# SSD stage of a hybrid SSD and chunk-MLP mixer: products from states in float32r parts, row tiles loaded by direction

## The chip, the cores and the metric

The kernel runs on one core of one Trainium2 chip. The metric is the device time in microseconds of one execution. The engines are named as in the profile: PE is TensorE (matmuls), PEld its weight loads, DVE VectorE, ACT ScalarE, POOL GpSimd, SP SyncE. L12 is line 12 of the kernel.

## The reference, cut to what matters

One layer of a mixer: a joint input projection of 256 latent and 256 context tokens (2,048 wide), a bidirectional SSD (32 heads of 64, in 8 groups of 4 heads, state 128, chunks of 128 tokens) beside a chunked gating MLP, and an output projection. Context tokens only provide the states from which the latent scans start. The part that the change touches, for one direction:

```
a = dtc * A;  acs = jnp.cumsum(a, axis=2);  a_tot = acs[:, :, -1]
decay_to_end = jnp.exp(a_tot[:, :, None] - acs)
states = einsum('bckgn,bckgr,bckgrp->bcgrpn', Bc, decay_to_end, xdt)
hT, h_starts = lax.scan(step, h0, (states, a_tot))     # h * exp(at) + s
CB = einsum('bcqgn,bckgn->bcgqk', Cc, Bc)
Lmat = exp(where(mask, acs_q - acs_k, -inf))
y_diag = einsum('bcgqk,bcgrqk,bckgrp->bcqgrp', CB, Lmat, xdt)
y_off = einsum('bcqgn,bcgrpn,bcqgr->bcqgrp', Cc, h_starts, exp(acs))
```

x, B and C come out of the projection through a depthwise convolution of 5 taps and silu. All is float32.

## The kernel before

The kernel has four stages one after another: adaLN and the first tiles of the projection (to about 126 us), the **SSD stage** (to about 440 us), the latent blocks, and the output projection. The change touches the SSD stage alone.

**Weight tiles.** The stage walks over 25 tiles of the projection (`REST`, i = 4 to 11, 14, 16 to 27, 30, 28, 29, 31), each of 128 output channels. Tile i belongs to group i // 4; i % 4 says what it holds: 0 and 1 are the two x tiles of the group, 2 is B, 3 is C (latent tokens only: 256 columns, the others 512). Tiles 12, 13 and 15 were computed earlier. One tile is 48 matmuls into a bank `psx` (two banks, used in turn): for each of 16 k steps three products in float32r parts, hi·hi (L140), hi·lo (L141) and lo·hi (L142). A weight tile is split in halves of 8 k steps, the hi part by ACT (`split_hi`, L542), the lo part by DVE (`split_lo`, L548, raw minus hi), three halves ahead of use. Halves are numbered through: tile 10 uses `w12` and `w13`.

**What sets the order.** Nothing is scheduled by the machine: each engine runs its instructions in the order in which the program issues them. Small jobs are put in a queue with a due time in units (`later`), and `pump` issues those that are due after each pair of k steps: 1.3 units for six matmuls of 512 columns, 0.65 for six of 256. So a due time fixes beside which matmuls of the projection a job stands, and on every engine the job waits behind what was issued before it. `plan_tile` (L975) gives the due times of a tile: tap 0 on ACT (L607), the other taps on DVE (L623), silu on ACT (L626), and what belongs to the group.

**A group's work**, in the order of due times after its C tile:

- `ssd_cb`: C by B for the latent chunks, PE into `pcb` (L851); `ssd_cbm`: its two masked copies `cbb` and `cbf` by DVE (L859, L860).
- `ssd_states`: context states, PE into `psc` (L868, B by the weighted x `xw`, two fp32 products of 512 columns), and states of the latent chunks into `psl` (L871).
- `ssd_hc` (ACT, L878, `hs` from `psc`), `ssd_hd` (POOL, L884), `ssd_hl` (DVE, L890): the start states `hs`.
- `ssd_mb` (POOL, L896) and `ssd_m` (DVE, L904 and L906), once per chunk: M, and E times M in place. M of the second chunk takes the buffer of the first, and yc that one again.
- `ssd_o`: C by `hs`, PE into `pso` (L920, two fp32 products of 512 columns); `ssd_yo` (DVE, L926) and `ssd_ya` (POOL, L934) take them out.
- `ssd_yd`: x by E, PE into `psy` (L946); `ssd_yc`, `ssd_yt`, `ssd_yf` turn it and add it to y.

**E.** `row_load` (POOL's DMA, L724) brings the running sums of a group, broadcast over 128 partitions, from DRAM (`acs`) into a tile `R` of 1 MB, both directions in one. ACT adds the negative column sums (`ssd_d`, L820), DVE takes the minimum of the two directions into a tile `E` (`ssd_min`, L827), ACT takes Exp (`ssd_e`, L833). This runs a group ahead: `plan_d` and `plan_e` are due 11 and 17 units after the C tile of the group before. Exp and silu lie in different tables of ACT, so each change costs an ACT_TABLE_LOAD.

`xw` and `xl` (x weighted for the states) are made by POOL (`ssd_w`, L785; `ssd_wl`, L792).

Of the kernel before, what the change touches and what calls it, by code (L numbers as in the profile page):

```python
# [47 lines left out]
def tile_hybrid_ssd_mlp(  # L48
# [688 lines left out]
    def turn(T, src, nm):
        nc.vector.transpose(T.rearrange("p (b g c) -> p g b c", b=4, g=4), src.rearrange("p (g b c) -> p g b c", g=4, b=4))
# [40 lines left out]
    def ssd_w(g):  # L779
        S = gs_[g]  # L780
        h4 = slice(4 * g, 4 * g + 4)
        xw = cv1.tile([P, 2, 2, 256], F32, tag="xw", name=f"xw{g}")
        for t in range(2):
            for d in range(2):
                nc.gpsimd.tensor_tensor(hx(xw[:, t, d, :]), xtok_(g, t), hb(wctx(t, d)[:, h4]), op=ALU.mult)  # L785
        S["xw"] = xw

    def ssd_wl(g):
        h4 = slice(4 * g, 4 * g + 4)
# [32 lines left out]

    def ssd_min(g, c):
        R = rows_[g]
        if c == 0:
            gs_.setdefault(g, {})["E"] = cv1.tile([P, 2, 4, P], F32, tag="E", name=f"E{g}")
        nc.vector.tensor_tensor(gs_[g]["E"][:, c], R[:, :, 0, c, :], R[:, :, 1, c, :], op=ALU.min)  # L827
        if c == 1:
            later(12 if g == 4 else 0, lambda: row_load(g + 1))

    def ssd_e(g):
# [1 line left out]
        nc.scalar.activation(E, E, AF.Exp)  # L833
# [28 lines left out]

    def ssd_states(g):
        S = gs_[g]
        bk, xw, xl = S["bk"], S["xw"], S["xl"]
        psc = spt([P, 2, 256], f"psc{g}")
        for t in range(2):
            nc.tensor.matmul(psc, lhsT=bk[:, t, :], rhs=xw[:, t], start=t == 0, stop=t == 1)  # L868
# [31 lines left out]
    def ssd_m(g, c):  # L900
        S = gs_[g]
        E, M = S["E"], S["M"]
        for h in range(4):
            nc.vector.scalar_tensor_tensor(M[:, h, :], S["cbf"][:, c, :], dtt[:, 3 * c, 4 * g + h : 4 * g + h + 1],  # L904
                                           M[:, h, :], op0=ALU.mult, op1=ALU.add)
        nc.vector.tensor_tensor(E[:, c], M, E[:, c], op=ALU.mult)  # L906
# [8 lines left out]
    def ssd_o(g):  # L915
        S = gs_[g]
        ct, hs = done[4 * g + 3], S["hs"]
        S["pso"] = [spt([P, 2, 256], f"pso{g}{c}") for c in range(2)]
        for c in range(2):
            nc.tensor.matmul(S["pso"][c], lhsT=ct[:, c * P : (c + 1) * P], rhs=hs[:, c], start=True, stop=True)  # L920
# [17 lines left out]
    def ssd_yd(g):  # L938
        S = gs_[g]
        E, xk = S["E"], S["xk"]  # L940
        ps = spt([P, 2, 2, P], f"psy{g}")
        for c in range(2):
            for q in range(2):
                for hh in range(2):
                    h = 2 * q + hh
                    nc.tensor.matmul(ps[64 * hh : 64 * hh + 64, c, q, :], lhsT=xk[:, q, 2 + c, hh * 64 : (hh + 1) * 64],  # L946
                                     rhs=E[:, c, h, :], start=True, stop=True)
# [467 lines left out]
```

## Time and profile before

| | |
|---|---|
| median of 3 runs | 962.25 us (961.64 to 963.29) |
| profiled execution, its own time | 962.39 us |
| its span | 960.6 us |
| granted clock | 0.998 |
| matmul records | 5,128 |

The page gives busy time of each engine over the span; the rows of the timeline give the start in us from the span's start, the duration, the engine with its line, the operation, output and inputs by name, the tile, and in brackets how long the engine had stood idle and what ended that. A row with x4 stands for four records run together. For the eight groups the timeline gives these starts of the products (us), and the end of the second E:

| group | pcb | psc | pso | second E done | psy |
|---|---|---|---|---|---|
| 0 | 169.1 | 169.5 | 178.9 | 184.5 | 184.9 |
| 1 | 196.0 | 196.5 | 205.9 | 207.8 | 211.8 |
| 2 | 241.7 | 242.2 | 251.6 | 253.0 | 258.9 |
| 3 | 269.6 | 270.0 | 279.7 | 281.6 | 285.7 |
| 4 | 303.1 | 303.6 | 311.6 | 314.9 | 318.9 |
| 5 | 347.6 | 348.0 | 356.1 | 358.7 | 363.3 |
| 6 | 392.0 | 392.5 | 400.5 | 403.8 | 407.8 |
| 7 | 422.0 | 422.4 | 432.7 | 437.3 | 438.6 |

### The profile page before, as it was taken

The page shows a single profiled execution, that of the slowest core. Times are in us where ns is not written, and L with a number is a line of the kernel's source. Part 1 is how long each engine was busy: PE and PEld are TensorE (multiplying, and loading weights), DVE is VectorE, ACT ScalarE, POOL GpSimd, SP SyncE. Part 2 cuts the span into 40 slices and gives each one's busy share as a digit, 9 for nine tenths or more (in the row PEclk, how much of TensorE's full clock was granted, in tenths as well). Part 3 has the DMA queues.
Part 4 walks back from the last instruction along what each step waited for, and adds up shares of the span by engine and source line. Part 5 has one row for each costly group of instructions (what it writes and reads, how often), then busy time and mean ns, then how long its engine had stood idle before and what let it go on. Part 6 is the DMA issues. An engine that isn't in the chain of part 4 may idle for free.

```text
span 960.6 us, 13754 instructions
## 1 busy us (share of the span) xinstructions
PE 950.8 (99%) x5128; PEld 769.6 (80%) x5128; DVE 675.0 (70%) x1108; ACT 481.8 (50%) x728; POOL 192.1 (20%) x294
## 2 busy tenths in 40 slices
PE   9999999999999999999999999999999999999997
PEld 4688888778787878787888888888888888888885
DVE  6888899889787776676766776766666665445636
ACT  4344358565564544455445443455665554355522
POOL 0000002423424324243000000043445440000000
PEclk9999999999999999999999999999999999999999
DMA  9999967468668667467787777786666666556722
GB/s 366 418 415 416 365 232 203 124 167 190 168 148 224 146 205 160 143 180 258 296 304 283 261 275 294 269 304 215 220 219 211 228 211 215 186 190 243 267 88 87
DMA packets 149970, 225.63 MB, mean 235 GB/s; under 512 B 119296, under 2 KB 119552, under 8 KB 127248
## 3 DMA queue, kind: packets, MB, share of 16 engines
q1 hardware_dynamic: 142992, 207.08, 64.0%
q0 software_dynamic: 6336, 16.86, 5.3%
q8 instruction: 40, 0.66, 0.3%
q10 hardware_dynamic: 576, 0.82, 0.2%
q14 instruction: 26, 0.21, 0.1%
HBM read 211.29 MB, written 9.25 MB: 230 GB/s over the span
## 4 chain that ended last, share of the span: by engine, by line
PE 93%; DVE 3%; DMA 2%; issue 1%; POOL 1%; ACT 0%; SPq 0%; POOLq 0%; ACTq 0%
PE pa L1192 12%; PE pa L1191 12%; PE pa L1193 12%; PE psx L140 9%; PE psx L142 9%; PE psx L141 9%; PE pm L1232 3%; PE pm L1233 3%; PE pm L1234 3%; PE pq L1234 2%; PE pq L1232 2%; PE pq L1233 2%; PE psada L253 2%; DMA ada<-in_wada_dram 1%; PE pso L920 1%; PE psc L868 1%
## 5 line engine op out<-in xcount | busy, mean ns | idle before, releaser
L87 DVE TENSOR_TENSOR lo_w<-w,hi_w 128x1024 fp32r<-128x1024 f32 x173 | 209.8, 1221 | 133.8 <-ACT hi_w L86 133.7
L86 ACT CAST hi_w<-w 128x1024 fp32r<-128x1024 f32 x173 | 181.9, 1053 | 206.4 <-PE pa L1193 138.1
L1191 PE MATMUL pa<-hi_w,hhi 128*128 128x512 f32 x512 | 200.5, 392 | 0.0
L1193 PE MATMUL pa<-hi_w,hlo 128*128 128x512 f32 x512 | 199.3, 389 | 0.0
L1192 PE MATMUL pa<-lo_w,hhi 128*128 128x512 f32 x512 | 199.2, 389 | 0.0
L140 PE MATMUL psx<-hhi,hi_w 128*128 128x512 f32 (+1 forms) x400 | 151.3, 378 | 1.0 <-DVE xbc L623 1.0
L142 PE MATMUL psx<-hhi,lo_w 128*128 128x512 f32 (+1 forms) x400 | 145.6, 364 | 0.0
L141 PE MATMUL psx<-hlo,hi_w 128*128 128x512 f32 (+1 forms) x400 | 145.6, 364 | 0.0
L1191 PEld LDWEIGHTS pa<-hi_w,hhi 128*128 128x128 f32 x512 | 96.1, 188 | 20.2 <-issue 0.4
L1193 PEld LDWEIGHTS pa<-hi_w,hlo 128*128 128x128 f32 x512 | 96.1, 188 | 20.0
L1192 PEld LDWEIGHTS pa<-lo_w,hhi 128*128 128x128 f32 x512 | 96.1, 188 | 19.9 <-issue 0.2
L548 DVE TENSOR_TENSOR lo_w<-w,hi_w 128x1024 fp32r<-128x1024 f32 x61 | 76.9, 1268 | 17.1 <-ACT hi_w L542 17.0
L623 DVE SCALAR_TENSOR_TENSOR xbc<-psx,pc,xbc 128x248 f32<-128x248 f32 (+1 forms) x204 | 83.3, 471 | 7.7 <-ACT xbc L607 6.9
L140 PEld LDWEIGHTS psx<-hhi,hi_w 128*128 128x128 f32 x400 | 75.4, 189 | 15.5 <-issue 3.1
L141 PEld LDWEIGHTS psx<-hlo,hi_w 128*128 128x128 f32 x400 | 75.5, 189 | 13.0 <-issue 1.7
L542 ACT CAST hi_w<-w 128x1024 fp32r<-128x1024 f32 x61 | 63.4, 1043 | 44.6 <-PE psx L141 30.8
L142 PEld LDWEIGHTS psx<-hhi,lo_w 128*128 128x128 f32 x400 | 75.4, 189 | 12.2
L1232 PE MATMUL pm<-hi_w,hhi 128*128 128x512 f32 x128 | 49.8, 389 | 0.0
L1233 PE MATMUL pm<-lo_w,hhi 128*128 128x512 f32 x128 | 49.8, 389 | 0.0
L1234 PE MATMUL pm<-hi_w,hlo 128*128 128x512 f32 x128 | 49.8, 389 | 0.0
L1071 DVE SCALAR_TENSOR_TENSOR junk<-gate,cb 128x2048 bf16<-128x2048 f32 x16 | 36.6, 2291 | 18.4 <-DMA gate<-in_wada_dram 18.4
L1096 POOL DMA_DIRECT2D y<-T x64 | 36.9, 584 | 47.6 <-ACT sq L1167 32.6
(268 smaller groups left out, 1405.7 us busy)
## 6 DMA issues: line engine op xcount, KB each, us to landing
w<-in_wlat_dram SPq DMA_DIRECT2D x64, 1024.0 KB, 4.9
w<-in_wout_dram SPq DMA_DIRECT2D x32, 1024.0 KB, 4.8
w<-in_wxbc_dram SPq DMA_DIRECT2D x25, 1024.0 KB, 6.6
ada<-in_wada_dram SPq DMA_DIRECT2D x24, 1024.0 KB, 13.7
gate<-in_wada_dram SPq DMA_DIRECT2D x16, 1024.0 KB, 5.4
ada<-in_wada_dram SPq DMA_DIRECT2D x16, 512.0 KB, 12.4
R<-acs POOLq DMA_DIRECT2D x8, 1024.0 KB, 7.2
wst<-in_wst_dram SPq DMA_DIRECT2D x15, 480.0 KB, 12.9
```

The source lines that it names most:

```text
L86: nc.scalar.copy(hi, raw)
L87: nc.vector.tensor_tensor(lo, raw, hi.bitcast(F32), op=ALU.subtract)
L140: nc.tensor.matmul(ps, lhsT=whi, rhs=hhi[k][:, s], start=start, stop=False)
L141: nc.tensor.matmul(ps, lhsT=whi, rhs=hlo[k][:, s], start=False, stop=False)
L142: nc.tensor.matmul(ps, lhsT=wlo, rhs=hhi[k][:, s], start=False, stop=stop)
L623: nc.vector.scalar_tensor_tensor(ao, zi, cw[:, k : k + 1], ao, op0=ALU.mult, op1=ALU.add)
L1191: nc.tensor.matmul(pa[tk], lhsT=hhi[k][:, t], rhs=whi[:, w], start=k == 0, stop=False)
L1192: nc.tensor.matmul(pa[tk], lhsT=hhi[k][:, t], rhs=wlo[:, w], start=False, stop=False)
L1193: nc.tensor.matmul(pa[tk], lhsT=hlo[k][:, t], rhs=whi[:, w], start=False, stop=k == KT - 1)
L1232: nc.tensor.matmul(p, lhsT=yh[:, t], rhs=whi[:, w], start=j == 0, stop=False)
L1233: nc.tensor.matmul(p, lhsT=yh[:, t], rhs=wlo[:, w], start=False, stop=False)
L1234: nc.tensor.matmul(p, lhsT=yl[:, t], rhs=whi[:, w], start=False, stop=hf == 0 and j == 15)
```

## The change

1. **Rows by direction.** `acs` holds the two directions apart, and `row_load(g, d)` fills one of two tiles R0, R1 of 512 KB. There is no tile E: the minimum and Exp are written in place in R0. R1 of the next group is loaded after the minima, R0 only after psy of this group. The biases of R1 are due at 11 units as before, those of R0 at 24, the minima and Exp at 28.5 (before 17).
2. **States** of groups 1 to 6 as three float32r products: `xw` and B are split by a new `hi_lo` (ACT copy to the hi part, L800 of the new file; DVE subtracts it for the lo part, L801).
3. **Outputs from states** of groups 1, 2, 4, 5, 6 as three float32r products: C and `hs` are split in the same way. Their pso, yo and ya are due 8 units later, behind psy.
4. **Due times**: `late` of tile 7 is 18 (14), of tile 15 it is 20 (17); in group 1 `xl` and the skip term come 3 later, in group 3 `xw` 1.5 later.

The diff, cut to its core:

```diff
-        R = cv1.tile([P, 4, 2, 2, P], F32, tag="R", name=f"R{g}")
...
+        R = cv1.tile([P, 4, 2, P], F32, tag=f"R{d}", name=f"R{d}_{g}")
+        nc.gpsimd.dma_start(R.rearrange("p h c q -> p (h c q)"),
+                            acs[d, 4 * g : 4 * g + 4, :].rearrange("h x -> (h x)").unsqueeze(0).partition_broadcast(P))
+        rows_[g, d] = R
...
+    def out_parts(g):
+        return g in (1, 2, 4, 5, 6)
+
+    def state_parts(g):
+        return 0 < g < NGRP - 1
...
+    def hi_lo(hi, lo, raw):
+        nc.scalar.copy(hi, raw)
+        nc.vector.tensor_tensor(lo, raw, hi.bitcast(F32), op=ALU.subtract)
...
+        hi_lo(S["xp"][0][:, t], S["xp"][1][:, t], S["xr", t])
...
+        hi_lo(bp[:, 0], bp[:, 1], S["bk"][:, 0:2])
...
+        hi_lo(cp[:, 0], cp[:, 1], done[4 * g + 3])
...
+        hi_lo(*S["hp"], S["hs"])
...
+        R = rows_[g, 0]
+        gs_.setdefault(g, {})["E"] = R
+        nc.vector.tensor_tensor(R[:, :, c, :], R[:, :, c, :], rows_[g, 1][:, :, c, :], op=ALU.min)
         if c == 1:
-            later(12 if g == 4 else 0, lambda: row_load(g + 1))
+            later(LATER_B.get(g, 0), lambda: row_load(g + 1, 1))
...
-            nc.tensor.matmul(psc, lhsT=bk[:, t, :], rhs=xw[:, t], start=t == 0, stop=t == 1)
+            if state_parts(g):
+                nc.tensor.matmul(psc, lhsT=bh, rhs=xh, start=t == 0, stop=False)
+                nc.tensor.matmul(psc, lhsT=bh, rhs=xo, start=False, stop=False)
+                nc.tensor.matmul(psc, lhsT=bl, rhs=xh, start=False, stop=t == 1)
...
-            nc.tensor.matmul(S["pso"][c], lhsT=ct[:, c * P : (c + 1) * P], rhs=hs[:, c], start=True, stop=True)
+            if out_parts(g):
+                nc.tensor.matmul(p, lhsT=ch, rhs=hh, start=True, stop=False)
+                nc.tensor.matmul(p, lhsT=ch, rhs=hl, start=False, stop=False)
+                nc.tensor.matmul(p, lhsT=cl, rhs=hh, start=False, stop=True)
...
-            late = max(late, 17.0 if i == 15 else 14.0)
+            late = max(late, {7: 18.0, 15: 20.0}.get(i, 14.0))
...
+            tp = TP if out_parts(g) else 0.0
-                          (12, ssd_o), (12.2, lambda g: ssd_m(g, 1)), (13.9, lambda g: ssd_yo(g, 0)),
+                          (12 + tp, ssd_o), (12.2, lambda g: ssd_m(g, 1)), (13.9 + tp, lambda g: ssd_yo(g, 0)),
...
+                          (16 + td, ssd_yd), (16.9 + td, ssd_yc), (17.2 + td, lambda g: row_load(g + 1, 0)),
...
+            if out_parts(g):
+                later(d0 + 7.2, lambda: ssd_cp(g))
+                later(d0 + 10.6, lambda: ssd_hp(g))
-            plan_d(d0 + 11, g + 1, 1.5)
-            plan_e(d0 + 17, g + 1)
+            plan_d(d0 + 11, g + 1, 1.5, 1)
+            plan_d(d0 + 24 + td, g + 1, 1.0, 0)
+            plan_e(d0 + 28.5 + td, g + 1)
...
+    WP, BP, TP = 3.0, 14.5, 8.0
```

What the due times do to the order is seen best in group 1. A number behind a tile's name is its group or tile, the one behind the underscore only a running number. **TensorE, between weight tiles 9 and 10**, before:

```order
L142 MATMUL psx9_2049<-hhi15_131,lo_w11_1934 128x512
L851 MATMUL pcb1_2149<-xbc7_1911,xbc6_1830 128x128 x2
L868 MATMUL psc1_2152<-xw1_1981,bk1_1953 128x512 x2
L871 MATMUL psl1_2155<-xl1_2024,bk1_1953 128x256 x2
L140 MATMUL psx10_2158<-hhi0_116,hi_w12_1979 128x512
```

and of the changed kernel, 18 matmuls of tile 10 later:

```order
L142 MATMUL psx10_2155<-hhi5_121,lo_w12_1996 128x512
L890 MATMUL pcb1_2196<-xbc7_1913,xbc6_1832 128x128 x2
L910 MATMUL psc1_2199<-xwh1_2023,bp1_2140 128x512
L911 MATMUL psc1_2199<-xwl1_2024,bp1_2140 128x512
L912 MATMUL psc1_2199<-xwh1_2023,bp1_2140 128x512
...
L917 MATMUL psl1_2206<-xl1_2075,bk1_1955 128x256 x2
L140 MATMUL psx10_2155<-hhi6_122,hi_w12_1981 128x512
```

The three products of group 1 moved from the seam of two tiles into tile 10, and psc became two times three matmuls (the second three are left out). Further on, the order before is 30 matmuls of tile 10, pso1, 18 of tile 10, psy1, tile 11; now it is 30 of tile 10, 30 of tile 11, psy1, 18 of tile 11, 12 of tile 14, pso1.

**ScalarE, around tap 0 of tile 9** (L607 with `psx9`), before:

```order
L833 ACT_TABLE_LOAD
L833 ACTIVATE E1_2081<-E1_2081 128x1024
L626 ACT_TABLE_LOAD
L626 ACTIVATE xbc8_2056<-xbc8_2056 128x512
L542 CAST hi_w14_2122<-w7_1868 128x1024
L607 ACTIVATE xbc9_2165<-psx9_2049,pc_87 128x512
L542 CAST hi_w15_2167<-w7_1868 128x1024
L878 COPY hs1_2187<-psc1_2152 128x2x256
L820 ACTIVATE R2_2092<-R2_2092,y_68 128x128 x4
L626 ACTIVATE xbc9_2165<-xbc9_2165 128x512
L542 CAST hi_w16_2237<-w8_1977 128x1024
```

and of the changed kernel:

```order
L607 ACTIVATE xbc9_2162<-psx9_2047,pc_87 128x512
L542 CAST hi_w15_2164<-w7_1870 128x1024
L858 ACTIVATE R0_1_2088<-R0_1_2088,y_68 128x128 x2
L870 ACT_TABLE_LOAD
L870 ACTIVATE R0_1_2088<-R0_1_2088 128x1024
L800 CAST cp1_2222<-xbc7_1913 128x256
L626 ACT_TABLE_LOAD
L626 ACTIVATE xbc9_2162<-xbc9_2162 128x512
L924 COPY hs1_2234<-psc1_2199 128x2x256
L542 CAST hi_w16_2238<-w8_1979 128x1024
L607 ACTIVATE xbc12_2240<-y_68,pc_87 128x512
L800 CAST hsh1_2277<-hs1_2234 128x1024
```

Exp of group 1 (E1, now in R0) moved from ahead of this tap to behind it, ahead of the copy of `hs` and of the hi half of weight 16; the casts of C (`cp1`) and `hs` (`hsh1`) are new.

**VectorE, from the lo half of weight 15 on**, before:

```order
L548 TENSOR_TENSOR lo_w15_2195<-w7_1868,hi_w15_2167 128x1024
L890 TENSOR_TENSOR hs1_2187<-psl1_2155,hs1_2187 128x256 x2
L904 SCALAR_TENSOR_TENSOR M10_2173<-cbf1_2169,dtt_1459,M10_2173 128x128 x4
L906 TENSOR_TENSOR E1_2081<-M10_2173,E1_2081 128x512
L904 SCALAR_TENSOR_TENSOR M11_2222<-cbf1_2169,dtt_1459,M11_2222 128x128 x4
L906 TENSOR_TENSOR E1_2081<-M11_2222,E1_2081 128x512
L548 TENSOR_TENSOR lo_w16_2256<-w8_1977,hi_w16_2237 128x1024
```

and of the changed kernel (left out are the eight taps of tile 12):

```order
L548 TENSOR_TENSOR lo_w15_2186<-w7_1870,hi_w15_2164 128x1024
L864 TENSOR_TENSOR R0_1_2088<-R0_1_2088,R1_1_1738 128x4x128 x2
L898 TENSOR_TENSOR cbb1_2218<-pcb1_2196,tri_ge_99 128x256
L899 TENSOR_TENSOR cbf1_2217<-pcb1_2196,tri_le_96 128x256
L801 TENSOR_TENSOR cp1_2222<-xbc7_1913,cp1_2222 128x256
L548 TENSOR_TENSOR lo_w16_2250<-w8_1979,hi_w16_2238 128x1024
L936 TENSOR_TENSOR hs1_2234<-psl1_2206,hs1_2234 128x256 x2
...
L950 SCALAR_TENSOR_TENSOR M10_2225<-cbf1_2217,dtt_1459,M10_2225 128x128 x4
L952 TENSOR_TENSOR R0_1_2088<-M10_2225,R0_1_2088 128x4x128
L746 STREAM_TRANSPOSE tx21_2267<-xbc9_2162 128x4x4x32
L801 TENSOR_TENSOR hsl1_2278<-hs1_2234,hsh1_2277 128x1024
```

The minima of group 1 (L864) stand in this row now, the lo half of weight 16 moved ahead of the adds to `hs`, and the taps of tile 12, a transpose and the subtraction for `hs` stand between those adds and the second M and E, which follow the last row.

More of the change, by code (lines that the diff above doesn't have):

```diff
@@ L637, in tile_hybrid_ssd_mlp @@
     arow = yseg(6)[0:32].rearrange("p (a q) -> p a q", a=4)
-    acs = drp.tile([32, 4 * P], F32, name="acs")
+    acs = drp.tile([2, 32, 2 * P], F32, name="acs")
     eu = ed.rearrange("p (u h) -> p u h", h=32)
@@ L708, in dt_out @@
     def dt_out():
-        nc.gpsimd.dma_start(acs, arow.rearrange("h a q -> h (a q)"))
-        row_load(0)
+        for d in range(2):
+            nc.gpsimd.dma_start(acs[d], arow[:, 2 * d : 2 * d + 2].rearrange("h c q -> h (c q)"))
+        row_load(0, 1)
+        row_load(0, 0)
     def dt_cols():
@@ L833, in ssd_e, with plan_d @@
         nc.scalar.activation(E, E, AF.Exp)
-    def plan_d(d0, g, step):
+    LATER_B = {}
+    def plan_d(d0, g, step, d):
         if g < NGRP:
             for n in range(4):
-                later(d0 + n * step, lambda n=n: ssd_d(g, n // 2, 2 * (n % 2)))
+                later(d0 + n * step, lambda n=n: ssd_d(g, d, n // 2, 2 * (n % 2)))
     def plan_e(d0, g):
@@ L864, in ssd_states @@
         S = gs_[g]
-        bk, xw, xl = S["bk"], S["xw"], S["xl"]
+        bk, xl = S["bk"], S["xl"]
         psc = spt([P, 2, 256], f"psc{g}")
         for t in range(2):
-            nc.tensor.matmul(psc, lhsT=bk[:, t, :], rhs=xw[:, t], start=t == 0, stop=t == 1)
+            if state_parts(g):
+                bh, bl = (S["bp"][:, i, t] for i in range(2))
+                xh, xo = (p[:, t] for p in S["xp"])
+                nc.tensor.matmul(psc, lhsT=bh, rhs=xh, start=t == 0, stop=False)
+                nc.tensor.matmul(psc, lhsT=bh, rhs=xo, start=False, stop=False)
+                nc.tensor.matmul(psc, lhsT=bl, rhs=xh, start=False, stop=t == 1)
+            else:
+                nc.tensor.matmul(psc, lhsT=bk[:, t, :], rhs=S["xw"][:, t], start=t == 0, stop=t == 1)
         psl = spt([P, 2, 256], f"psl{g}")
@@ L919, in ssd_o @@
         for c in range(2):
-            nc.tensor.matmul(S["pso"][c], lhsT=ct[:, c * P : (c + 1) * P], rhs=hs[:, c], start=True, stop=True)
+            p, cs = S["pso"][c], slice(c * P, (c + 1) * P)
+            if out_parts(g):
+                ch, cl = (S["cp"][:, i, cs] for i in range(2))
+                hh, hl = (q[:, c] for q in S["hp"])
+                nc.tensor.matmul(p, lhsT=ch, rhs=hh, start=True, stop=False)
+                nc.tensor.matmul(p, lhsT=ch, rhs=hl, start=False, stop=False)
+                nc.tensor.matmul(p, lhsT=cl, rhs=hh, start=False, stop=True)
+            else:
+                nc.tensor.matmul(p, lhsT=ct[:, cs], rhs=hs[:, c], start=True, stop=True)
     def ssd_yo(g, c):
@@ L988, in plan_tile @@
             late_w = lx == LAND
-            later(d0 + tx + tw, lambda: ssd_w(g))
-            later(d0 + tx + tw + (3 if late_w else 0), lambda: ssd_wl(g))
-            later(d0 + tx + tw + (6 if late_w else 3), lambda: ssd_sk(g))
+            if state_parts(g):
+                WS = 1.5 * (g == 3)
+                for t in range(2):
+                    later(d0 + tx + tw + 1.3 * t + WS, lambda t=t: ssd_w(g, t))
+                    later(d0 + tx + tw + WP + 1.5 * t + WS, lambda t=t: ssd_wp(g, t))
+            else:
+                later(d0 + tx + tw, lambda: ssd_w(g))
+            later(d0 + tx + tw + (3 if late_w else 0) + 3 * (g == 1), lambda: ssd_wl(g))
+            later(d0 + tx + tw + (6 if late_w else 3) + 3 * (g == 1), lambda: ssd_sk(g))
         if r == 2:
```

60 lines of the change are left out of this document (36 added, 24 removed).

## The prediction

> **What bounds the kernel now.** I read the page's span, its first part and its chain first, then the rows of the one place in the SSD stage where TensorE stands still.
>
> ```profile
> span 960.6 us, 13754 instructions
> ...
> PE 950.8 (99%) x5128; PEld 769.6 (80%) x5128; DVE 675.0 (70%) x1108; ACT 481.8 (50%) x728; POOL 192.1 (20%) x294
> ...
> PE 93%; DVE 3%; DMA 2%; issue 1%; POOL 1%; ACT 0%; SPq 0%; POOLq 0%; ACTq 0%
> ```
> ```profile
> 219.90 0.47 PE L140 MATMUL psx<-hhi,hi_w 128*128 128x512 f32 x1 [1.04 <-DVE xbc L623]
> ```
> PE is busy 99% of the span and makes 93% of the chain. So time goes in two ways only: PE gets fewer passes, or PE waits. The one long wait of the stage is 1.04 us at 219.90, for the taps of tile 10, which still hold its bank. The neighbours are not idle either, stretch by stretch (PE, PEld, DVE, ACT, POOL busy us):
>
> ```profile
> 196.00:220.00 24.00, 22.96 (x130) 18.35 (x130) 22.71 (x49) 14.45 (x27) 7.50 (x9) 1.00 0.61 145
> 220.00:260.00 40.00, 40.00 (x183) 31.60 (x183) 32.81 (x62) 21.09 (x39) 14.40 (x19) 1.00 0.78 188
> ```
> In group 1's stretch DVE is busy 22.71 of 24 us, in group 2's 32.81 of 40. Work put on DVE there has little room. The sum is made against the profiled run, 962.39 us (1.8 outside the span of 960.6); the median of the three runs is 962.25, so the two are the same for this purpose.
>
> **What the passes save.** An old product against the new form:
>
> ```profile
> 176.00 0.39 PE L142 MATMUL psx<-hhi,lo_w 128*128 128x512 f32 x1
> ...
> 178.72 0.39 PE L142 MATMUL psx<-hhi,lo_w 128*128 128x512 f32 x1
> 178.94 1.88 PE L920 MATMUL pso<-hs,xbc 128*128 128x512 f32 x4
> ...
> 180.89 0.40 PE L141 MATMUL psx<-hlo,hi_w 128*128 128x512 f32 x1
> ```
> From 176.00 to 178.72 lie 12 matmuls in float32r parts: 0.227 us each. pso starts at 178.94; its successor, one matmul before 180.89, starts at 180.66. So two fp32 products of 512 columns cost 1.72 us, and as six float32r ones 6 x 0.227 = 1.36. That saves 0.36 for each pair, in 6 groups for psc and 5 for pso: 11 x 0.36 = **-3.9**. The bank wait goes with the order, since in group 1 PE gets to tile 14 after psy1 (below): **-1.0**. [...]
>
> **What is paid for it: group 1.** Rows of the same stretch in the kernel before, first TensorE, then ScalarE, then VectorE and GpSimd:
>
> ```profile
> 196.05 0.60 PE L851 MATMUL pcb<-xbc,xbc 128*128 128x128 f32 x4
> 196.49 1.88 PE L868 MATMUL psc<-xw,bk 128*128 128x512 f32 x4
> ...
> 198.89 0.58 PE L140 MATMUL psx<-hhi,hi_w 128*128 128x512 f32 x1
> ...
> 211.83 1.09 PE L946 MATMUL psy<-E,xk 128*64 128x128 f32 x16
> ...
> 213.07 0.28 PE L141 MATMUL psx<-hlo,hi_w 128*128 128x256 f32 x1
> ...
> 213.90 0.28 PE L142 MATMUL psx<-hhi,lo_w 128*128 128x256 f32 x1
> ```
> ```profile
> 196.25 0.78 ACT L607 ACTIVATE xbc<-psx,pc 128x512 f32<-128x512 f32 x1 [0.67 <-PE psx L142]
> ...
> 198.41 0.59 ACT L878 COPY hs<-psc 128x512 f32<-128x512 f32 x1 [0.45 <-PE psc L868]
> ...
> 218.02 1.06 ACT L833 ACTIVATE E<-E 128x1024 f32<-128x1024 f32 x1
> 219.10 1.28 ACT L626 ACT_TABLE_LOAD   x1
> 220.39 0.63 ACT L626 ACTIVATE xbc<-xbc 128x512 f32<-128x512 f32 x1
> 220.93 1.03 ACT L542 CAST hi_w<-w 128x1024 fp32r<-128x1024 f32 x1
> ```
> ```profile
> 198.02 3.17 DVE L623 SCALAR_TENSOR_TENSOR xbc<-psx,pc,xbc 128x248 f32<-128x248 f32 x8
> 201.11 1.21 DVE L548 TENSOR_TENSOR lo_w<-w,hi_w 128x1024 fp32r<-128x1024 f32 x1
> 202.24 0.75 DVE L890 TENSOR_TENSOR hs<-psl,hs 128x256 f32<-128x256 f32 x2
> 202.91 1.13 DVE L904 SCALAR_TENSOR_TENSOR M<-cbf,dtt,M 128x128 f32<-128x128 f32 x4
> 204.07 0.69 DVE L906 TENSOR_TENSOR E<-M,E 128x512 f32<-128x512 f32 x1
> ...
> 207.16 0.69 DVE L906 TENSOR_TENSOR E<-M,E 128x512 f32<-128x512 f32 x1
> ...
> 212.04 0.70 DVE L738 STREAM_TRANSPOSE tx<-xbc 128x512 f32<-128x512 f32 x1
> ...
> 409.60 1.25 DVE L827 TENSOR_TENSOR E<-R 128x512 f32<-128x512 f32 x2
> ```
> ```profile
> 204.91 1.04 POOL L896 TENSOR_TENSOR M<-cbb,dtt 128x512 f32<-128x512 f32 x1 [4.64 <-DVE E L906]
> ```
> **PE's side.** Before, E1 is done at 207.16 + 0.69 = 207.85 and psy1 starts at 211.83: 4.0 us to spare. In the new order PE ends tile 9 at 196.05, runs 18 matmuls of tile 10 (4.1), pcb (0.44), psc as six (1.36), psl (198.89 - 196.49 - 1.72 = 0.68), 30 matmuls of tile 10 (6.8) and 30 of tile 11 at 256 columns (7 steps from 213.07 to 213.90, so 0.12 each: 3.6). It stands before psy1 at **213.0**.
>
> **The other side.** Tap 0 of tile 9 ends at 197.0, its other taps run to 200.2, the lo half of weight tile 15 to 201.4, the two minima of group 1 (1.25) to 202.6, Exp (1.06) to 203.7. These minima and this Exp ran well ahead of group 1's own products before; now they stand between them. Behind Exp ACT has the copy of C (no row; 256 elements where silu has 512 in 0.63, so between 0 and 0.63; I take 0.4), the table load (1.28), silu of tile 9 (0.63), the copy of hs (0.59) and the hi half of weight tile 16 (1.03): 207.6. DVE's next instructions are cbb, cbf and the lo part of C, then the lo half of weight 16, which waits for that hi half. All behind it waits too: DVE, short of time in this stretch, stands idle for 3.9 us. Then come lo of weight 16 (1.2), the adds to hs (0.7), taps of tile 12 (3.15), M (1.13), E (0.69), a transpose (0.70), the new subtraction for hs (1,024 elements as lo_w: 1.22), M and E again (1.8). That is 218.2; the rows overlap a little (201.11 + 1.21 is 0.08 past 202.24), which takes 0.2 off: E1 at **218.0**. So psy1 waits **+5.0**. Its floor, if DVE lost nothing to ACT, is 5.0 - 3.9 = 1.1; its top depends on the rows of group 1. They are loaded only after psy of group 0 now, and the biases of row tile R0 stand ahead of tap 0 of tile 9:
>
> ```profile
> R<-acs POOLq DMA_DIRECT2D x8, 1024.0 KB, 7.2
> ```
> I issue it at about 189.9 (behind psy0 and POOL's adds to y) and let 512 KB take 4.8, two thirds of the 7.2 of 1,024 KB; with the full 7.2 all of it comes 2.4 later, so the stall is 1.1 to 7.4.
>
> **Groups 3 to 6.** Group 3's states come with Exp of its own rows ahead of the copy of hs on ACT. Exp with its table load costs 1.06 + 1.28 = 2.34 there at most, nothing if PE's 18 matmuls of tile 20 cover it; no row shows it, and I take the middle, **+1.0**. For groups 4 to 6 group 6 stands as the example:
>
> ```profile
> 393.35 3.19 DVE L623 SCALAR_TENSOR_TENSOR xbc<-psx,pc,xbc 128x248 f32<-128x248 f32 x8
> ...
> 401.92 1.14 DVE L904 SCALAR_TENSOR_TENSOR M<-cbf,dtt,M 128x128 f32<-128x128 f32 x4 [1.22 <-POOL M L896]
> 403.10 0.69 DVE L906 TENSOR_TENSOR E<-M,E 128x512 f32<-128x512 f32 x1
> ```
> ```profile
> 407.81 1.09 PE L946 MATMUL psy<-E,xk 128*64 128x128 f32 x16
> ```
> E1 is done at 403.79, psy starts at 407.81: 4.0 to spare. PE comes 2.1 earlier now (pso, 1.72, has moved behind psy, and psc saves 0.36). The lo part of C stands ahead of the taps at 393.35 and waits for ACT's copy: about 1.35 later. The subtraction for hs (1.22) fits the gap of 1.22 in which DVE waits for POOL's M. That leaves 4.0 - 2.1 - 1.35 = 0.55. But the two meet there: POOL's M starts when the first E ends, and so does DVE's subtraction, and rows show what a meeting costs:
>
> ```profile
> 223.49 2.33 POOL L785 TENSOR_TENSOR xw<-xk,ed 128x256 f32<-128x256 f32 x4 [5.70 <-DMA yz<-Dy]
> ...
> 418.74 5.22 POOL L785 TENSOR_TENSOR xw<-xk,ed 128x256 f32<-128x256 f32 x4 [9.49 <-ACT xk L766]
> ```
> The same four products take 2.33 us on POOL at 223.49 and 5.22 at 418.74, where DVE computes differences of weights. So one waits out the other, M's 1.04: 0.55 - 1.0 is 0.44 late in each of three groups, **+1.3** (0 without the meeting), and in group 1 a partial meeting of **+0.5** (0 to 1.0). [...]
>
> Other edits I cost at nothing. The 512 KB row loads and the later yo and ya lie on queues and engines off PE's path; if that cover goes, POOL's adds hold the next R0 as above. The splits of xw and B (1,280 elements on ACT and DVE) come before their products while PE works on weight tiles; uncovered they would cost 1.5 in a group, and that is the rival of the backlog. Group 7 keeps its products.
>
> **Sum:** -3.9 - 1.0 + 5.0 + 0.5 + 1.0 + 1.3 = +2.9, so 962.39 + 2.9 = **965.3**.
>
> **The rivals.** *Faster:* in group 1 DVE doesn't stand idle, since ACT gets to weight half 16 in time. It decides at 204.5, when DVE has the lo part of C behind it: with that hi half done by then the stall is 1.1, group 3 and the meetings vanish too, and 962.39 - 3.9 - 1.0 + 1.1 = 958.6. Against it stands the order: Exp, table load, silu and the copy of hs are queued ahead of that half. *No meetings:* POOL and DVE pass each other: without 1.3 and 0.5, 963.5. Against it: 5.22 against 2.33. *Backlog:* the 5 us of group 1 are still on DVE when group 2 begins, whose window has 7.2 us free and gets 3.2 more work (2,560 elements by 1.22 per 1,024). Nothing is left over, and psy2 is late by up to 3.2: 968.5, and with late rows 2.4 more, 971. *No cheaper products:* the parts cost what fp32 did: 965.3 + 3.9 = 969.2; the cadence of 0.227 speaks against it.
>
> **How the numbers follow.** Forecast 0.35, faster 0.27, no meetings 0.20, backlog 0.14, no cheaper products 0.04. 0.2% is 1.9 us, about what a measurement of this kernel tells from no change: faster is below 960.3, slower above 964.2. Of the forecast (its own range 963 to 967.5) 0.07 lies within, of no meetings 0.17. So faster 0.27, same 0.24, slower 0.28 + 0.03 + 0.14 + 0.04 = 0.49. The range goes from no stall at all (962.39 - 4.9 = 957.5) to the backlog with late rows, 971.
>
> **What would show it.** In the changed profile: psc and pso as six rows 0.227 apart; psy1 with about 5 us of idle time before it, released by DVE's last E; DVE idle some 4 us before the lo half of weight 16, with Exp and a table load on ACT beside it; psy of groups 4 to 6 starting with less than a microsecond to spare or waiting; no 1.04 before tile 14. It is wrong if psy1 doesn't wait, if the R0 rows hold ACT rather than Exp, or if PE waits at weight halves, where I count nothing.

## The result and the profile after

| kernel | median us | runs |
|---|---|---|
| before | 961.94 | 4 (961.6 to 963.29) |
| changed | 983.31 | 4 (982.79 to 984.7) |

The changed kernel is slower: ratio 1.0222, 95% interval 1.0204 to 1.0239. The profiled run took 984.70 us, 22.3 more than that of before. The page of the changed kernel (span, busy time by engine, granted clock in 40 slices):

```profile
span 982.8 us, 13889 instructions
...
PE 954.7 (97%) x5150; PEld 777.4 (79%) x5150; DVE 701.9 (71%) x1136; ACT 495.6 (50%) x756; POOL 205.9 (21%) x303
...
PEclk9999999989999999999999999999999999999999
```

PE's share fell from 99% to 97%, and the ninth slice, which holds group 1, has a clock of 8 tenths where before all had 9 or more. The view of what PE waited for says where (total us, times, longest):

```profile
PE psy L1000 <- DVE R L952: 8.3, 4, 3.2
PE pso L974 <- DVE hs L936: 4.4, 1, 4.4
PE pa L1262 <- DVE lo_w L87: 2.2, 2, 1.5
PE psc L910 <- ACT bp L800: 1.8, 2, 0.9
...
PE psc L914 <- POOL xw L797: 1.4, 1, 1.4
...
PE psy L1000 <- ACT R L858: 1.1, 1, 1.1
```

These make 19.2 us. Before, the two waits of the same kind were 1.04 (tile 14) and 0.54 (psc of group 7), so **17.6 us are new waits**. Group 1 first, in the timeline of the changed kernel, TensorE, ScalarE and VectorE:

```profile
214.67 0.66 PE L1000 MATMUL psy<-R,xk 128*64 128x128 f32 x8 [1.12 <-ACT R L858]
218.56 1.12 PE L1000 MATMUL psy<-R,xk 128*64 128x128 f32 x8 [3.23 <-DVE R L952]
```
```profile
202.76 1.06 ACT L870 ACTIVATE R<-R 128x1024 f32<-128x1024 f32 x1 [2.77 <-DVE R L864]
...
204.13 1.28 ACT L626 ACT_TABLE_LOAD   x1
205.43 0.63 ACT L626 ACTIVATE xbc<-xbc 128x512 f32<-128x512 f32 x1
205.96 0.57 ACT L924 COPY hs<-psc 128x512 f32<-128x512 f32 x1
206.43 1.05 ACT L542 CAST hi_w<-w 128x1024 fp32r<-128x1024 f32 x1
```
```profile
207.51 1.37 DVE L548 TENSOR_TENSOR lo_w<-w,hi_w 128x1024 fp32r<-128x1024 f32 x1 [2.53 <-ACT hi_w L542]
...
215.00 1.72 DVE L801 TENSOR_TENSOR hsl<-hs,hsh 128x1024 fp32r<-128x1024 f32 x1
...
217.81 0.69 DVE L952 TENSOR_TENSOR R<-M,R 128x512 f32<-128x512 f32 x1
```

psy needs E chunk by chunk: its first half waits 1.12 us, its second 3.23. E is done at 217.81 + 0.69 = 218.50; DVE gets the lo half of weight 16 only at 207.51, since its hi half stands on ACT behind Exp, the table load, silu and the copy of hs; and the subtraction for hs stands ahead of the second E.

The second thing is what a wait does to PE afterwards. Windows of 1 us (busy us of PE, PEld, DVE, ACT and POOL with counts, then the granted clock, DMA share, GB/s) behind group 1's wait, and then behind the waits of groups 3 and 4:

```profile
216.00:217.00 1.00, 0.00 (x0) 0.00 (x0) 1.00 (x3) 0.10 (x1) 0.00 (x0) 0.56 1.20 190
...
220.00:221.00 1.00, 1.00 (x6) 1.00 (x6) 1.00 (x4) 0.00 (x0) 0.58 (x1) 0.50 0.78 121
222.00:223.00 1.00, 1.00 (x7) 1.00 (x7) 1.00 (x2) 0.33 (x1) 0.00 (x0) 0.52 0.34 98
295.00:296.00 1.00, 1.00 (x3) 0.41 (x2) 1.00 (x2) 0.00 (x0) 0.47 (x1) 0.50 0.00 0
...
336.00:337.00 1.00, 1.00 (x7) 1.00 (x6) 1.00 (x3) 0.16 (x1) 0.23 (x1) 0.50 0.08 25
```

After waits of 3.23, 4.37 and 2.77 us the clock was 0.50 for some microseconds of work. Busy time of PE by one minus the clock, summed over all such windows, is 2.2 us behind group 1, 1.7 behind group 3 and 1.7 behind group 4: **5.6**.

What the parts save, in the changed kernel:

```profile
200.62 0.48 PE L910 MATMUL psc<-xwh,bp 128*128 128x512 f32 x1
200.94 0.40 PE L911 MATMUL psc<-xwl,bp 128*128 128x512 f32 x1
...
202.08 1.02 PE L917 MATMUL psl<-xl,bk 128*128 128x256 f32 x4
...
268.51 0.39 PE L970 MATMUL pso<-hsh,cp 128*128 128x512 f32 x1
...
269.88 0.39 PE L140 MATMUL psx<-hhi,hi_w 128*128 128x512 f32 x1
```

psc takes 1.46 us and pso 1.37, against 1.72 before: 6 x 0.26 + 5 x 0.35 = **3.3 us saved**. So 17.6 + 5.6 - 3.3 = 19.9 of the 22.3 us are accounted for. The 2.4 left are not assigned; a wait is counted from the modelled end of the matmul ahead, so part of it may lie at the eleven starts after a wait.

### The profile page after: what moved, and what is told of

Same layout as the page of the kernel before. It is cut to its first block, busy times and chain, and to the rows that moved or that the text cites. A ratio compares the mean times of both kernels' runs of the same rounds, so it can differ in the third digit from the quotient of the medians.

```text
span 982.8 us, 13889 instructions
## 1 busy us (share of the span) xinstructions
PE 954.7 (97%) x5150; PEld 777.4 (79%) x5150; DVE 701.9 (71%) x1136; ACT 495.6 (50%) x756; POOL 205.9 (21%) x303
## 4 chain that ended last, share of the span: by engine, by line
PE 45%; DMA 9%; DVE 4%; issue 2%; ACT 0%; POOL 0%; SPq 0%; DVEq 0%; ACTq 0%
PE pa L1262 8%; PE pa L1261 8%; PE pa L1263 8%; DMA gate<-in_wada_dram 8%; PE pm L1304 3%; PE pm L1302 3%; PE pm L1303 3%; PE pq L1304 2%; PE pq L1303 2%; PE pq L1302 2%; DVE lo_w L87 2%; PE psx L140 1%; PE psx L142 1%; PE psx L141 1%; DVE junk L1141 1%
```

## The experiments

Theory A: Exp in place in R0 can't run ahead, since R0 is held until psy of the group before; it stands on ACT amid a group's own products, and that makes the waits. Theory B: the splits are the load that ACT and DVE have no room for. Theory C: both, where the splits stand ahead of the second E. Each kernel ran once beside the kernel before, unless said otherwise; before took 961.77 to 961.89 beside them. Its 15 timed runs spread over 1.4 us, so a difference of single times below about 1.5 tells nothing.

**The row tiles without any parts.**

```diff
     def out_parts(g):
-        return g in (1, 2, 4, 5, 6)
+        return False
     def state_parts(g):
-        return 0 < g < NGRP - 1
+        return False
```

> The changed kernel with the two switches for the products in parts off: psc and pso of all groups are fp32 products again, nothing is split, no pso is delayed; the row tiles by direction, the late minima and Exp, and the new due times stay. Theory A (Exp in place in R0 comes too late and stands on ACT in the middle of a group's own products): most of the loss stays, 972 to 980 us, with PE waiting before psy or pso of groups 1, 3 and 4. Theory B (the splitting of xw, B, C and hs is what ACT and DVE have no room for): the loss goes, 961 to 965 us.

970.28 us: 8.5 above before, 13 below the changed kernel. Below A's 972, well above B's 965: the row tiles cost by themselves, but are not the whole. PE waited 1.13 us at psy and 0.80 at a bank of psx in group 1, 2.40 at psc of group 2, and 0.42 at pso of group 3.

**One kind of parts at a time**: only `out_parts` off (rows_states), and only `state_parts` off (rows_outs).

> The changed kernel with the products of states in parts but pso of all groups in fp32 at its old due time; C and hs aren't split. Theory A: as rows_only, less 6 x 0.36 = 2.2 us of passes, and the waits for the split B (0.9 in groups 2 and 4) back: 971 to 979. Theory B: the splits of C and hs were the trouble, so 961 to 966.

> The changed kernel with psc of all groups in fp32 (no split of xw and B), pso of five groups in parts and 8 units later. Theory A: as rows_only, less 5 x 0.33 = 1.6 us of passes: 967 to 971. Theory C: the splits of hs ahead of the second E come on top of the late Exp: 973 to 979, with waits before psy of groups 1, 2 and 4 as in the changed kernel.

974.09 and 978.15. Each kind makes the late rows dearer, by 3.8 and 7.9, though each takes PE passes away. In rows_states psc of group 2 waits 4.62 us for the parts of B; in rows_outs psy of group 1 waits 0.81 and 3.23, nearly as in the changed kernel: Theory C for that group, and the splits of xw and B are no part of its cause.

**The parts with Exp a group ahead.** R0 gets two buffers. The room comes from the lo parts: that of xw moves into the buffer of hs, those of hs into yo0 and yo1.

```diff
-        R = cv1.tile([P, 4, 2, P], F32, tag=f"R{d}", name=f"R{d}_{g}")
+        R = (cv1 if d else cv2).tile([P, 4, 2, P], F32, tag=f"R{d}", name=f"R{d}_{g}")
...
-            later(LATER_B.get(g, 0), lambda: row_load(g + 1, 1))
+            later(12 if g == 4 else 0, lambda: (row_load(g + 1, 1), row_load(g + 1, 0)))
...
-            plan_d(d0 + 24 + td, g + 1, 1.0, 0)
-            plan_e(d0 + 28.5 + td, g + 1)
+            plan_d(d0 + 11, g + 1, 1.5, 0)
+            plan_e(d0 + 17, g + 1)
```

> All products stay in parts, but R0 has two buffers (the lo parts of xw and hs take over buffers of hs and yo), so rows, minima and Exp of the next group run a group ahead as in the kernel before (biases at 11, Exp at 17 units). Theory A: the waits of group 1, 3 and 4 go and the passes are saved: 957 to 961 us. Theory B: the splits still hold ACT and DVE: 972 us or more, PE waiting at psy of groups 1, 2 and 4.

968.39: 15 us of the 21 go, and no window of the SSD stage has a clock below 1.00. But it isn't the 957 to 961 of Theory A: psy still waits 4.6 us in sum (2.50, 1.56 and 0.54).

**The price of the clock.** Extra matmuls ahead of the late products, into the bank that these then overwrite, keep PE busy through its waits:

```diff
+            for n in range({(1, 0): 9, (1, 1): 27, (2, 1): 14, (4, 1): 23}.get((g, c), 0)):
+                nc.tensor.matmul(ps[:, c].rearrange("p q k -> p (q k)"), lhsT=hhi[0][:, 0:P], rhs=hhi[1][:, 0:256], start=True, stop=True)
```

(and 19 of 512 columns ahead of pso of group 3).

> The changed kernel; PE runs extra matmuls, as long as its waits were in the trace (1.1 and 3.2 us ahead of the two halves of psy of group 1, 1.7 in group 2, 4.4 ahead of pso of group 3, 2.8 in group 4), into the bank that the product then overwrites. If the granted clock of 0.5 after those waits is a price of its own, it stays at 1.00 and the time falls by what the windows at a low clock lost, about 6 us: 976 to 978. If the low clock cost nothing, the time stays at 983.

980.24: 3.1 less than the changed kernel's median, not 6. The clock stays up in the same windows:

```profile
220.00:221.00 1.00, 1.00 (x11) 1.00 (x10) 1.00 (x3) 0.00 (x0) 0.05 (x1) 1.00 0.36 67
...
336.00:337.00 1.00, 1.00 (x10) 1.00 (x9) 1.00 (x4) 0.40 (x1) 0.00 (x0) 1.00 1.10 307
```

A faster PE runs into the next wait sooner: psc of groups 2 and 4 waits 1.31 and 1.65 us here, against 0.87 and 0.88 in the changed kernel. So the low clock costs some 3 us net; against the four single times of the changed kernel this one run stands 2.6 to 4.5 lower.

**The splits of C and hs behind the second E**: in the changed kernel (split_late), and with Exp ahead (early_split).

```diff
-                later(d0 + 7.2, lambda: ssd_cp(g))
-                later(d0 + 10.6, lambda: ssd_hp(g))
+                later(d0 + 13.0, lambda: ssd_cp(g))
+                later(d0 + 14.0, lambda: ssd_hp(g))
```

> The changed kernel with the splits of C and hs due at 13 and 14 units instead of 7.2 and 10.6, so that on DVE they stand behind the second E of their group and not ahead of it. Theory A (late Exp alone sets the waits before psy): the waits before psy stay where they were, 981 to 984 us. Theory C (the splits ahead of E add to the late Exp, and each wait over some 2.7 us costs the clock too): psy of groups 1, 2 and 4 waits 1.5 to 2 us less in each, two of the three drops of the clock go: 971 to 976.

> early_all with the splits of C and hs behind the second E as in split_late. Theory C: psy of groups 1, 2 and 6 waits no more than 1 us in sum (4.6 in early_all): 962 to 965 us. If the splits are not what is late there, it stays at 968.

974.93: **8.4 us less**, within the range of Theory C; the waits of psy in groups 2, 4 and 6 are gone, group 1 keeps 0.83 + 2.27, and pso of group 3 keeps 4.75. One drop of the clock goes, that of group 4, and not two: behind group 1 it falls here too, after a longest wait of 2.27. With Exp ahead the same move gives 967.92, no change that a single run can tell from early_all: psy of group 1 waits 1.46 instead of 2.50, but a bank of psx 1.74, and pso of group 3 1.48. That miss says that with Exp ahead something else holds the kernel.

**The C tiles of groups 1 and 3 at their old due times**, with Exp ahead and the splits late:

```diff
-            late = max(late, {7: 18.0, 15: 20.0}.get(i, 14.0))
+            late = max(late, 17.0 if i == 15 else 14.0)
```

> early_split with the due times of the C tiles of groups 1 and 3 of the kernel before (14 and 17 instead of 18 and 20). With Exp a group ahead nothing is left that the delay was needed for, PE runs psy where it did before: 957 to 961 us, about 3 below the kernel before for the passes, with psc of some groups waiting up to 1 us for the split B. If the splits need the delay, psc of group 1 waits for B and xw and it is 963 or more.

969.04: not the 957 to 961, but the other case, in which the splits need the delay. psy and pso don't wait at all now, but psc does, for the split B, 1.7 us in group 1, 3.95 in group 2 and 1.07 in group 3. Group 2 in the timeline of this kernel, POOL, ACT, DVE and PE, each alone:

```profile
231.70 1.19 POOL L797 TENSOR_TENSOR xr<-xk,ed 128x256 f32<-128x256 f32 x2 [3.94 <-DMA Dx<-tx]
```
```profile
232.91 0.62 ACT L800 CAST xwhp<-xr 128x512 fp32r<-128x512 f32 x1 [4.33 <-POOL xr L797]
```
```profile
233.57 0.69 DVE L801 TENSOR_TENSOR xwhs<-xr,xwhp 128x512 fp32r<-128x512 f32 x1 [4.10 <-ACT xwhp L800]
```
```profile
247.72 0.80 PE L914 MATMUL psc<-xwhp,bp 128*128 128x512 f32 x1 [3.95 <-ACT bp L800]
```

POOL waits for a DMA, ACT's cast for POOL, DVE's subtraction for ACT, and everything issued after it on ACT and DVE, the taps of the next tiles among it, waits in line. So the split of xw has brought a wait for a DMA into the two queues that feed PE. Which later wait of PE each of these makes was not taken apart; early_outs below takes both splits out.

**Group 3 and the parts of B.** In the changed kernel ACT stands idle in group 3 until POOL is done with the buffer that the parts of B take (the adds to y of group 2), and tap 0 of tile 18 stands behind. POOL, ACT, DVE and PE:

```profile
274.60 4.38 POOL L988 TENSOR_TENSOR y<-y,yo 128x256 f32<-128x256 f32 x4
```
```profile
279.00 0.41 ACT L800 CAST bp<-bk 128x256 fp32r<-128x256 f32 x1 [4.26 <-POOL y L988]
...
280.50 0.76 ACT L607 ACTIVATE xbc<-psx,pc 128x512 f32<-128x512 f32 x1
...
286.86 1.06 ACT L870 ACTIVATE R<-R 128x1024 f32<-128x1024 f32 x1 [1.83 <-DVE R L864]
...
288.41 1.28 ACT L626 ACT_TABLE_LOAD   x1
289.71 0.63 ACT L626 ACTIVATE xbc<-xbc 128x512 f32<-128x512 f32 x1
290.24 0.55 ACT L607 ACTIVATE xbc<-psx,pc 128x256 f32<-128x256 f32 x1
```
```profile
287.41 3.61 DVE L548 TENSOR_TENSOR lo_w<-w,hi_w 128x1024 fp32r<-128x1024 f32 x1
290.94 2.01 DVE L623 SCALAR_TENSOR_TENSOR xbc<-psx,pc,xbc 128x248 f32<-128x248 f32 x4
292.86 0.75 DVE L936 TENSOR_TENSOR hs<-psl,hs 128x256 f32<-128x256 f32 x2
```
```profile
293.76 2.89 PE L974 MATMUL pso<-hs,xbc 128*128 128x512 f32 x4 [4.37 <-DVE hs L936]
```

Either that wait or Exp could set the wait of pso. The test moves the cast:

```diff
-                later(d0 + tx + BP + 7.5 * (g == 3), lambda: ssd_bp(g))
+                later(d0 + tx + BP + 10.5 * (g == 3), lambda: ssd_bp(g))
```

> The changed kernel with one due time moved: the split of B of group 3 comes 3 units later, on ACT behind tap 0 of tile 18. In the changed kernel that cast stands 4.26 us waiting for POOL's add to y of group 2, which still reads the buffer yo1 that the parts of B take, and tap 0 of tile 18 stands behind it. Theory D (this wait in ACT's order, not Exp of group 3, makes pso of group 3 wait 4.37): tap 0 of tile 18 comes 3 to 4 us earlier, pso waits at most 1.5, the clock doesn't drop there: 976 to 980 us. If Exp sets it, pso of group 3 still waits 4 us and the time stays at 983.

984.23, and pso of group 3 still waits 4.71 us: the forecast of Theory D doesn't come. The rows of this kernel:

```profile
276.28 0.78 ACT L607 ACTIVATE xbc<-psx,pc 128x512 f32<-128x512 f32 x1 [0.62 <-PE psx L142]
...
285.41 1.28 ACT L870 ACT_TABLE_LOAD   x1 [5.30 <-DVE cbb L898]
286.71 1.06 ACT L870 ACTIVATE R<-R 128x1024 f32<-128x1024 f32 x1
```
```profile
279.19 0.42 DVE L801 TENSOR_TENSOR bp<-bk,bp 128x256 fp32r<-128x256 f32 x1 [1.97 <-ACT bp L800]
...
290.67 2.02 DVE L623 SCALAR_TENSOR_TENSOR xbc<-psx,pc,xbc 128x248 f32<-128x248 f32 x4 [3.82 <-ACT xbc L607]
```
```profile
293.49 3.33 PE L974 MATMUL pso<-hs,xbc 128*128 128x512 f32 x4 [4.71 <-DVE hs L936]
```

Tap 0 of tile 18 comes 4.2 us earlier, Exp 0.15, pso 0.27. Exp, two table loads and silu stand ahead of tap 0 of tile 19, the taps of tile 19 ahead of the adds to hs: DVE stands 3.82 us before those taps. But the edit doesn't take POOL's adds out of the way. The subtraction for B still stands on DVE ahead of the taps of tile 18 and still waits for the cast and, through it, for POOL; the taps and the minima behind them come only 1.8 us earlier. And the table load for Exp, which the changed kernel did while ACT waited for the minima, comes behind them here. So this kernel alone doesn't tell the wait for POOL from Exp.

The other kernels with a late Exp do. Group 3 in five of them (us):

| kernel | psc starts | Exp starts | pso starts | psc to Exp | Exp to pso | pso waits |
|---|---|---|---|---|---|---|
| rows_only | 277.48 | 280.02 | 286.91 | 2.54 | 6.89 | 0.42 |
| rows_states | 281.45 | 284.06 | 290.95 | 2.61 | 6.89 | 0.76 |
| rows_outs | 277.83 | 283.35 | 290.25 | 5.52 | 6.90 | 3.41 |
| changed | 280.63 | 286.86 | 293.76 | 6.23 | 6.90 | 4.37 |
| bp3_later | 280.04 | 286.71 | 293.49 | 6.67 | 6.78 | 4.71 |

What stands between Exp and pso takes the same 6.8 to 6.9 us everywhere, and in rows_only the work of PE covers all of it but 0.42. The wait grows with the start of Exp behind psc. rows_only and rows_outs differ in `out_parts` alone, and that takes the wait from 0.42 to 3.41. Exp and pso of rows_only, then the biases of R0 on ACT and pso of rows_outs:

```profile
280.02 1.06 ACT L870 ACTIVATE R<-R 128x1024 f32<-128x1024 f32 x1 [1.27 <-DVE R L864]
```
```profile
286.91 1.96 PE L974 MATMUL pso<-hs,xbc 128*128 128x512 f32 x4 [0.42 <-DVE hs L936]
```
```profile
275.22 1.87 ACT L858 ACTIVATE R<-R,y 128x128 f32<-128x128 f32 x6 [5.84 <-DMA R<-acs]
```
```profile
290.25 2.71 PE L974 MATMUL pso<-hs,xbc 128*128 128x512 f32 x4 [3.41 <-DVE hs L936]
```

With `out_parts` pso of group 2 comes 8 units later, and its adds on POOL with it. In rows_outs POOL stands idle 8.05 us until that pso is done and then makes xw of group 3, the load of R0 is issued behind it (269.79, against 264.90 in rows_only), and ACT stands 5.84 us for it ahead of tap 0 of tile 18. In the changed kernel POOL is done with these adds at 278.98 (262.68 in rows_only), and the cast of B stands 4.26 us for them, again ahead of that tap. Either way the taps, the minima and Exp of group 3 come later. That it is the delay of 8 units and not the splits of C and hs fits split_late, where these splits come later and pso waits 4.75; no kernel takes the delay away alone.

**Without the split of xw and B, or with it only where there is room.** From early_old: psc in parts for no group (early_outs); for groups 4 to 6 (early_s456); and psc and pso in parts for groups 4 to 6 alone (early_456).

> early_old with psc of all groups in fp32: no split of xw and B. If what is left of the loss there (psc of groups 1, 2 and 3 waiting for the parts of B) is the price of these two splits, the waits go and 5 x 0.33 us of passes are saved against the kernel before: 959 to 961 us. If R0 by direction or the splits of C and hs cost by themselves, 963 or more.

> early_outs with psc in parts for groups 4, 5 and 6 alone, where DVE was busy 31 of 44 us before: 3 x 0.25 us of passes more, 958 to 960.5 us. If the splits of xw and B cost as much there as in groups 1 to 3, it is above early_outs by 1 us or more.

> Products in parts only in groups 4, 5 and 6, psc and pso; groups 0 to 3 as before the change, save R0 by direction. Saves 3 x 0.25 + 3 x 0.33 = 1.7 us: 959.5 to 961. Groups 1 to 3 keep the wait of 1.0 at tile 14. If early_outs is faster, the parts pay in the crowded groups too.

960.42, 959.26 and 962.22. Taking the split of xw and B out of early_old is worth 8.6 us, and out of groups 1 to 3 alone 9.8. The first two are as expected; they differ by 1.2, which single runs don't separate, so the split in groups 4 to 6 neither costs nor pays as far as they tell. early_456 lies above its range and not below before: the parts of pso in groups 1 and 2 are not what costs. It stands 3.0 above early_s456, more than the passes of two pso (0.7); the rest is not explained.

**The row tiles alone, Exp ahead** (early_old without any parts):

> early_old without any product in parts: only the row tiles by direction with two buffers for R0, and E in place in R0; rows, minima and Exp a group ahead as before. If the lateness of Exp is the whole price of the row tiles, this is the kernel before within 1 us: 961 to 963, against 970.3 of rows_only. If loading by direction or Exp in place cost by themselves (twice as many DMA issues on POOL), it is 965 or more.

963.10 against 970.28 of rows_only, at the upper end of the range. It stands 1.2 us above before, which a single run doesn't tell from nothing: loading by direction and working in place cost little. That Exp is late, and the two C tiles with it, costs 7.

**The version that beats both**, early_s456 in five rounds:

> early_s456 again, timed in rounds: its one time of 959.26 stood 2.5 us below the kernel before beside it. If that holds, a ratio of 0.996 to 0.998 with an interval that excludes 1; if it was the scatter of single times, an interval that holds 1.

960.17 us (959.62 to 960.87, 11 runs) against 961.89 (15 runs): ratio 0.9982, interval 0.9973 to 0.9991. The single 959.26 was a little lucky; the gain is 1.7 us. What PE waited for in it:

```profile
PE psx L140 <- DVE xbc L623: 1.1, 2, 0.8
PE psc L918 <- POOL xw L797: 0.5, 1, 0.5
```

The waits are those of before, the passes fewer: 3 x 0.26 + 5 x 0.35 = 2.5, of which 1.7 arrive.

## Why the prediction was wrong

Forecast were 965.3 us and a range of 957.5 to 971; measured were 983.31. Three steps failed: the term of group 3, which became the longest single wait, with the later yo and ya that were costed at nothing; the splits of xw and B, costed at nothing; and what a wait does to the clock behind it, which no term has.

**Passes (-3.9): right, a little large.** 3.3 by the rows. A pso costs what was worked out (1.37), psc takes 0.1 more, since its first matmul behind pcb is followed after 0.32 us and not 0.227.

**The bank wait at tile 14 (-1.0): right**; it isn't among the waits.

**Group 1 (+5.0): right.** Forecast were PE at psy at 213.0, E done at 218.0, and DVE idle 3.9 us behind Exp, table load, silu, copy and hi half. Measured: E done at 218.50, waits of 1.12 + 3.23 = 4.35, DVE idle 2.53 us before that lo half. The meeting with POOL (+0.5) is there too: the subtraction for hs took 1.72 us instead of 1.22. Removing Exp from there left 2.50 (early_all), moving the split of hs as well 1.46, and giving the C tile its old due time back 0 at psy (in early_old at the price of 1.7 at psc, in early_outs without it). So the stall has three parts, and all of them stand in the prediction's sum, though Exp has less of it than thought: the sum leaves 1.1 without the idle time behind Exp, early_all 2.50. The third is not free to choose: Exp of group 1 is due at 31 + 28.5 + 2 = 61.5 units (group 0's C tile at 29 + 2, Exp 2 behind the minima); its first M and E are due at 36.4 + 18 + 9.5 = 63.9, tile 7 being called after 3 x 10.4 + 5.2 = 36.4 units. With 14 it would be 59.9, ahead of Exp. The late Exp forces the delay.

**What a wait costs behind itself (nothing): failed.** No term of the sum has PE at half its clock. 5.6 us by the windows, some 3 net by fill. The trace of before does not show it in this stage, where its longest wait was 1.04 us.

**Group 3 (+1.0), and the later yo and ya (nothing): failed, and this is the longest wait.** 4.37 us. The step said that Exp with its table load costs 2.34 there at most, nothing if the matmuls of tile 20 cover it, and took the middle. More than that stands between Exp and pso (a second table load, silu, tap 0 of tile 19 on ACT, then the taps of tile 19 and the adds to hs on DVE): 6.9 us. Still PE covers nearly all of it in rows_only, where pso waits 0.42. What the step had wrong is where Exp stands. It has Exp at its place in the order with nothing that makes it late, while the later pso of group 2 and its adds, which the prediction put off PE's path at no cost, hold POOL, then ACT and DVE, and Exp starts 6.23 us behind psc instead of 2.54. Switching on `out_parts` alone takes the wait from 0.42 to 3.41 (rows_only, rows_outs); the path over POOL is read from the rows and was not tested by itself. The kernels with Exp ahead wait 0.76, 1.48 and 0 there. The lo half at 287.41 took 3.61 us instead of 1.22, while POOL ran M and the decay of hs; that costs little here, as in bp3_later, where it took 1.21, the taps behind it start only 0.27 earlier.

**Groups 4 to 6 (+1.3) and group 2 (0): mis-sized.** psy waited 1.68 us in group 2, 2.77 in group 4, nothing in 5 and 0.65 in 6. Group 2 was only named as a rival (the backlog, up to 3.2). The mechanism, a split ahead of the second E where slack is short, is shown by split_late, where all three waits go.

**Splits of xw and B (nothing): failed.** "They come before their products while PE works on weight tiles" counted their duration, 1.5 us if uncovered. In line they hold more: psc waited 0.87 and 0.88 in the changed kernel, 4.62 in rows_states, 3.95 in early_old. Taking them out is worth 5.2 us in the changed kernel (rows_outs) and 8.6 once Exp is ahead.

**Not in the sum** were 2.2 us in the latent blocks, where PE waits for lo halves, and 0.9 more at psc of group 7. No experiment was made on these.

The prediction's range ended at 971 because the terms that failed were priced by the late instruction's own time and all terms were added. The runs show that the two halves of the change make each other dearer: the rows alone cost 8.5 us, the parts with Exp ahead 6.6 (early_all) or 7.3 (early_old), both together 21.4 and not 15 to 16.

## What to carry to other kernels

Price a moved instruction by what is queued behind it on its engine, and follow that queue until it reaches the engine that bounds. Do the same for what stands ahead of it: a product that is moved to a later place keeps its buffers longer, and here that moved Exp of the next group. A split that needs a result of a DMA or of POOL (waits of 3.94 and 4.33 us in early_old) belongs where its engine's queue can stand still; here the same splits cost some 9 us in three crowded groups and nothing that the runs can tell in three roomy ones. If two buffers are merged to make room, look first for the work that ran ahead because there were two.

## What the hardware showed

**The clock after a wait.** The granted clock was 0.50 behind waits of PE of 2.77, 3.23 and 4.37 us (changed kernel), 3.41 (rows_outs), 3.95 (early_old) and 4.62 (rows_states), and behind 2.50 (early_all), 2.60 (rows_outs) and 2.67 (bp3_later) no window shows it below 1.00 in that stretch. But the length of a wait didn't decide it in these runs. It was also low behind 2.27 us in split_late, with a wait of 0.83 just before, and behind 1.44 in bp3_later (group 7, with 0.37 just before). One window of split_late:

```profile
219.00:220.00 1.00, 1.00 (x7) 1.00 (x6) 1.00 (x4) 0.00 (x0) 0.00 (x0) 0.50 0.94 140
```

Each of the twelve drops in this stage, in all kernels together, lasts 3.4 us (eight of them) or 6.8 (four). Those of the changed kernel start at 216.13, 294.64 and 335.60, that is 78.51 and 40.96 us apart, 23.0 and 12.0 times 3.41. In the 3.41 us ahead of them PE was busy 1.48, 0.87 and 1.15 us. If the stage of this kernel is cut into stretches of 3.41 us counted from these starts, PE was busy 0.98 us in the first half of the long drop, which went on behind it, and 1.57 in the stretch from 287.81, behind which the clock stayed at 1.00; all others up to 445 us have 2.23 or more. In split_late the matmuls of 256 columns start 0.21 us apart up to 221.61, and 0.12 ahead of the waits; so the 3.4 us of that drop begin at about 218.3, and the wait of 2.27 lies whole in the 3.41 us ahead of it, in which PE was busy 1.14. In rows_outs the wait of 2.60, behind which there was no drop, lies in two such stretches, counted from its drop at 291.28, with PE busy about 1.9 and 2.3 us. What sets the clock the runs don't show. Half of 3.41 us is 1.7, so by estimate such a stretch at 0.50 costs PE at most that.

**VectorE beside GpSimd.** A lo half of 1.22 us took 3.61 at 287.41 while POOL ran 1.05 and 1.18 us: 1.22 + 1.05 + 1.18 = 3.45. In rows_only, beside the same two, it took 3.60.
